# Forgetting attention: weights turned by TensorE transposes in place of a second set of logits, and a TensorE order written out by hand

## The chip, the cores and the metric

One core of one Trainium2 chip runs the whole program. The metric is the device time in microseconds (us), as a median over runs; one further execution was recorded by the hardware profiler.

## What is computed

A decoder trunk of two layers over 1024 positions of 1024 features, all in fp32: a gated linear recurrence (RG-LRU), then forgetting attention (FoX) with 16 heads of 64, each with a residual, and an RMS norm at the end. The change is in the second layer:

```python
u = h @ w_in                            # q, k, v, gate (1024 each), f_logit (16)
cum = cumsum(log_sigmoid(f_logit + b_f))            # per head, over positions
logits = (q @ k.T) / 8 + cum[query] - cum[key]      # per head, causal mask
o = softmax(logits) @ v
x = x + (o * silu(gate)) @ w_out
return rms_norm(x, final_g)
```

## The kernel before

**Number format.** Every fp32 operand is split into a high and a low part (fp32r tiles with names in h and l, by `to_hi` L72 and `to_lo` L85), and a product is three matmuls: high by high, high by low, low by high (`gemm_steps` L105). Weights arrive by DMA as `wf`; ScalarE (ACT) casts the high part `wh`, GpSimd (POOL) subtracts for the low part `wl` (`weights` L99).

**First layer** (L160 to L461). It is not touched, except that matmuls are now called through a wrapper.

**Attention, per head `hd`.** Positions are cut into two halves `c` of 512 and eight blocks of 128. `T` holds the head's keys and `U` its queries (with high part, low part and the sums `cum` stacked along the partitions, so that two matmuls give a logit with its decay); `load` L559 fills them by DMA from the projections `qkh`, `qkl`.
- `maxima(hd, c)` L631: for each of four query blocks, two to four matmuls L654 and L655 give the logits `S` (queries on partitions, keys along the free axis) in PSUM; VectorE (DVE) adds the mask and takes the negated row maximum (L659); ACT takes the exponential with that bias, in place, for the row sums alone (L662). Then the four maxima are transposed (`mrow` L668) and DVE writes them into four rows of `U` (L669), so that a second product can subtract them.
- `weigh(hd, c)` L701: for each pair of key blocks the logits are computed once more, transposed (`ST`, keys on partitions, L723 and L724), ACT takes the exponential `p` (L729, L732), POOL zeroes what lies above the diagonal (L737), DVE makes `ph` (L81) and `pl` (L86), and TensorE (PE) adds `ph` and `pl` times the values into `O` (L757, L758). A last step adds the two halves of `O` (`yo`).
- `scale`, `gated` L696, L766: POOL multiplies by the reciprocal sums (which go through DRAM, `recd` to `recb`) and by the gate.

**PSUM.** Its eight banks are two buffers for projections (tag g), two for `O`, `mrow` and `tr` (tag O), and two of two banks each (tag S), which `S` and `ST` share: every new `S` or `ST` waits until the last reader of the one before the last has ended.

**Order.** `run(order, weigh, maxima, fill)` L786 steps through a string: 0 takes a step of `weigh`, 1 a step of `maxima`, a dot a step of `fill`, which is six matmuls of the projections for the next pair of heads (`kq_units` L538, `g_units` L618; for the last heads `partial` L811, the output product of the first six pairs). ORDERS L28 holds the strings. The fill is held behind the logits of LAG steps earlier, and otherwise a scheduler in the compiler orders each engine. The engines run what they were given in that order.

**The end.** `partial` adds into the residual `x1d` in DRAM; `turned(c, q)` L827 transposes the residual with four transposes per 128x512 tile (`turn` L850), adds the last two pairs' output product (L854 to L856), and takes squares, norm and scale.

Of the kernel before, what the change touches and what calls it, by code (L numbers as in the profile page):

```python
# [38 lines left out]
def trunk(ctx: ExitStack, tc: tile.TileContext, xt, w0, wg, wo0, pc, gn, gf, w1, wv, wf, bf, wo1, out):  # L39
# [10 lines left out]


# [11 lines left out]
    for _ in range(10):  # L63
        nc.tensor.matmul(warm[:, :P], onesf, onesf, start=True, stop=True)
# [40 lines left out]
    def gemm_steps(ps, pairs, chunks=(slice(0, HALF),)):  # L105

        pairs = list(pairs)
        for cs in chunks:
            o = ps[:, cs]
            for i, ((wh, wl), (xh, xl)) in enumerate(pairs):  # L110
                nc.tensor.matmul(o, wh, xh[:, cs], start=i == 0, stop=False)  # L111
                nc.tensor.matmul(o, wl, xh[:, cs], start=False, stop=False)  # L112
                nc.tensor.matmul(o, wh, xl[:, cs], start=False, stop=i == len(pairs) - 1)  # L113
                if i % 2:
                    yield
# [12 lines left out]
    def inv_rms(parts, col, rs, rms=None):  # L128

        nb = rs.shape[1] // P  # L130
        for b, i in itertools.product(range(nb), range(len(parts))):
            sq = parts[i][:, b * P : (b + 1) * P]
            nc.tensor.matmul(col[:, b : b + 1], sq, onesf[:, :1], start=i == 0, stop=i == len(parts) - 1)
# [7 lines left out]
        inst = nc.tensor.matmul(row, onesf, rs, start=True, stop=True)  # L141
# [23 lines left out]
    with ExitStack() as l0:  # L165
# [255 lines left out]
        def mm3(o, w, x, start, stop):  # L421
            (wh, wl), (xh, xl) = w, x
            nc.tensor.matmul(o, wh, xh, start=start, stop=False)
            nc.tensor.matmul(o, wl, xh, start=False, stop=False)
            nc.tensor.matmul(o, wh, xl, start=False, stop=stop)
# [35 lines left out]
    with ExitStack() as l1:  # L461
# [4 lines left out]
        own = tu.tile([4, 4, P], BF16, name="own")  # L466
        nc.gpsimd.memset(own, 0.0)
        nc.gpsimd.affine_select(
            out=own, in_=own, pattern=[[1, 4], [0, P]], compare_op=ALU.not_equal, fill=1.0, base=0, channel_multiplier=-1
        )  # L470


# [9 lines left out]
        U = [tu.tile([P, 2, SEQ], F32R, tag=f"U{s}", name=f"U{s}") for s in range(2)]  # L482
        for s in range(2):
            nc.gpsimd.memset(f32(T[s][64:, 1]), 1.0)
            nc.vector.memset(f32(U[s][64:, 1]), 0.0)
            nc.vector.memset(f32(U[s][64:68, 1]), -1.0)

        def project(cb_i, use, hs=(0, 1)):

            w = list(weights(w1[cb_i]))  # L490
# [6 lines left out]
        def values(g):  # L497
# [9 lines left out]
            for st in range(8):  # L507
# [5 lines left out]
                for k in range(KT):  # L513
# [3 lines left out]
                    nc.tensor.matmul(pt, xh, wh, start=k == 0, stop=False)  # L517
                    nc.tensor.matmul(pt, xl, wh, start=False, stop=False)  # L518
                    nc.tensor.matmul(pt, xh, wl, start=False, stop=k == KT - 1)  # L519
# [16 lines left out]
        y1 = [[], []]  # L536

        def kq_units(pair, hs=(0, 1)):  # L538

            for is_k in (1, 0):  # L540
                if hs[0] == 0:
                    kq[pair, is_k] = tuple(
                        kqpool.tile([P, SEQ], F32R, tag=f"qk{p}{is_k}", name=f"qk{p}") for p in "hl"
                    )
                hi, lo = kq[pair, is_k]
                eng = nc.vector if pair == 0 else nc.scalar

                def use(h, pt):
                    cs = slice(h * HALF, (h + 1) * HALF)
# [7 lines left out]
                yield from project(is_k * 8 + pair, use, hs)  # L557

        def load(hd, cs=slice(0, SEQ)):  # L559

            pair, s = hd // 2, hd % 2
            rows = slice(s * HD, (s + 1) * HD)
            for is_k, A in ((1, T[s]), (0, U[s])):
                hi, lo = (f32(z[rows, cs]) for z in kq[pair, is_k])
                nc.sync.dma_start(f32(A[:64, 0, cs]), hi)
                if is_k:
                    nc.sync.dma_start(f32(A[:64, 1, cs]), hi)
                    nc.sync.dma_start(f32(A[64:, 0, cs]), lo)
                else:
                    nc.sync.dma_start(f32(A[64:, 0, cs]), hi)  # L570
                    nc.sync.dma_start(f32(A[:64, 1, cs]), lo)
            nc.sync.dma_start(f32(T[s][66:68, 1, cs]), cumd[hd, :, cs])
            nc.sync.dma_start(f32(U[s][64:66, 1, cs]), cumd[hd, :, cs])


        drain(kq_units(0, (0,)))
# [6 lines left out]
        z = at.tile([HEADS, SEQ], F32, tag="p", name="z")  # L583
        e = at.tile([HEADS, SEQ], F32, tag="p", name="e")
# [3 lines left out]
        parts = [at.tile([HEADS, SEQ], F32R, tag=t, name="cp") for t in ("ph", "pl")]  # L588

        def forget(half):  # L590
            cs = slice(half * HALF, (half + 1) * HALF)
            pt = ps.tile([P, HALF], F32, tag="O", name="fps")
            for i in range(4):
                nc.tensor.transpose(pt[:HEADS, i * P : (i + 1) * P], fz[:, half * 4 + i], ident)
            z_, e_, hi, lo = z[:, cs], e[:, cs], *(c[:, cs] for c in parts)
# [10 lines left out]
            for i in range(2):  # L606
                nc.sync.dma_start(cumd[:, i, cs], f32(parts[i][:, cs]))
            for hd in range(2):
                if half == 0:
                    load(hd, cs)  # L610
# [7 lines left out]
        def g_units(pair):  # L618

            sg = sgs[pair] = at.tile([P, SEQ], F32, tag="sg", name="sg1")  # L620
# [6 lines left out]
            yield from project(16 + pair, use)  # L627

        stats = {}

        def maxima(hd, c):  # L631

            pair, s = hd // 2, hd % 2
            if c == 0:
                stats[hd] = (
                    at.tile([P, 8], F32R, tag="st", name="st"),  # L640
                    at.tile([P, 8], F32, tag="sums", name="sums"),
                )
            st, sums = stats[hd]
            for i in range(4 * c, 4 * c + 4):
# [4 lines left out]
                qs = slice(i * P, n)  # L649
                for lo_, hi_ in ((0, min(n, HALF - o_)), (HALF - o_, n)):  # L650
                    if hi_ <= lo_:
                        continue
                    hi_ = max(hi_, lo_ + 256)
                    nc.tensor.matmul(S[:, lo_:hi_], U[s][:, 0, qs], T[s][:, 0, lo_:hi_], start=True, stop=False)  # L654
                    last[0] = nc.tensor.matmul(  # L655
                        S[:, lo_:hi_], U[s][:96, 1, qs], T[s][:96, 1, lo_:hi_], start=False, stop=True
                    )
                m = st[:, i : i + 1]
                nc.vector.tensor_tensor_reduce(  # L659
                    S[:, :n], S[:, :n], mask[:, SEQ - n :], -1.0, -NEG, ALU.add, ALU.min, accum_out=m  # L660
                )
                seen[0] = nc.scalar.activation(  # L662
                    S[:, :n], S[:, :n], AF.Exp, bias=f32(m), scale=-1.0, accum_out=sums[:, i : i + 1]
                )
                yield

            pt = ps.tile([P, P], F32, tag="O", name="mrow")
            nc.tensor.transpose(pt[:4], f32(st[:, 4 * c : 4 * c + 4]), ident)  # L668
            nc.vector.tensor_tensor(  # L669
                U[s][96:100, 1, c * HALF : (c + 1) * HALF].rearrange("p (a b) -> p a b", a=4),  # L670
                pt[:4].unsqueeze(1).to_broadcast([4, 4, P]),
                own,
                ALU.mult,
            )
            yield
# [25 lines left out]
        def weigh(hd, c, sub=slice(0, HALF)):  # L701
# [8 lines left out]
            nj = end // P  # L710
            for j0 in range(0, nj, 2):
                A = ps.tile([P, 2, HALF], F32, tag="S", name="ST")
                p = at.tile([P, 2, HALF], F32, tag="p", name="p")
                ph = at.tile([P, 2, HALF], F32R, tag="ph", name="ph")
                pl = at.tile([P, 2, HALF], F32R, tag="pl", name="pl")
                qlo = []
                for jj in range(2):
                    j = j0 + jj
                    q0 = min(max(begin, j * P), end - 256)
                    qlo.append(q0)  # L720
                    n = end - q0
                    ks = slice(j * P, (j + 1) * P)
                    nc.tensor.matmul(A[:, jj, :n], T[s][:, 0, ks], U[s][:, 0, q0:end], start=True, stop=False)  # L723
                    last[0] = nc.tensor.matmul(  # L724
                        A[:, jj, :n], T[s][:, 1, ks], U[s][:, 1, q0:end], start=False, stop=True
                    )
                ns = [end - q for q in qlo]
                if ns[0] == ns[1]:
                    nc.scalar.activation(p[:, :, : ns[0]], A[:, :, : ns[0]], AF.Exp)  # L729
                else:  # L730
                    for jj in range(2):
                        nc.scalar.activation(p[:, jj, : ns[jj]], A[:, jj, : ns[jj]], AF.Exp)  # L732
                for jj in range(2):
                    j = j0 + jj
                    w = (j + 1) * P - qlo[jj]
                    if w > 0:
                        nc.gpsimd.affine_select(  # L737
                            out=p[:, jj, :w],
                            in_=p[:, jj, :w],
                            pattern=[[1, w]],  # L740
                            compare_op=ALU.is_ge,
                            fill=0.0,
                            base=qlo[jj] - j * P,
                            channel_multiplier=-1,
                        )
                if ns[0] == ns[1]:
                    rng = [(slice(0, 2), ns[0])]
                else:
                    rng = [(jj, ns[jj]) for jj in range(2)]
                for sl, n in rng:  # L750
                    to_hi(ph[:, sl, :n], p[:, sl, :n], nc.vector)
                    to_lo(pl[:, sl, :n], p[:, sl, :n], ph[:, sl, :n], nc.vector)
# [266 lines left out]
```

## Time and profile before

| | us |
|---|---|
| median of 3 runs (1154.35 to 1156.48) | 1155.97 |
| the profiled execution's own time | 1159.8 |
| its span, first to last instruction | 1157.9 |
| PE busy | 1131.8 |
| DVE, ACT, POOL busy | 818.3, 590.7, 311.0 |

The profiled execution is 3.8 us above the median, and 1.9 us of it lie outside the span. A matmul's end is modelled, and the next one starts before it: the time that a matmul takes from the engine is therefore read from one start to the next in the timeline, not from its length. PEclk in a row of the stretches view is the granted TensorE clock, 1.00 being full speed.

### The profile page before, as it was taken

Reading aid. Unit: us, or ns where it says so; the run is one execution under the profiler, and the core shown is the slowest. Engines: PE = TensorE matmul, PEld = TensorE weight load, DVE = VectorE, ACT = ScalarE, POOL = GpSimd, SP = SyncE. Lnnn points to the kernel's source line nnn. Section 1 sums busy time; section 2 is a strip of 40 time slices with the busy share of each in tenths; the row PEclk is TensorE's granted clock in tenths of the full one; section 3 lists DMA queues with packets and bytes.
Section 4 is the critical chain, followed back from the end, with each engine's and each line's share of the span. In section 5 each row is a group of like instructions: output and inputs, shape, how many; then the busy total and the mean of one; then the engine's idle time right before and its main releaser. Section 6 shows DMA issues by size and latency. Waiting matters only on the chain.

```text
span 1157.9 us, 15580 instructions
## 1 busy us (share of the span) xinstructions
PE 1131.8 (98%) x5565; PEld 944.8 (82%) x5565; DVE 818.3 (71%) x1294; ACT 590.7 (51%) x1009; POOL 311.0 (27%) x305
## 2 busy tenths in 40 slices
PE   9999999999999999999999999999999999999897
PEld 7787888888888887978888988889888898777685
DVE  7589766677566889556877757777577775577754
ACT  8388345345544656454554545545454454445323
POOL 1212212112021103342332333323333233141310
PEclk9999999999999999999999999999999999999898
DMA  6111111111111124351343323433234331646244
GB/s 211 51 41 50 51 51 55 42 50 41 51 59 37 55 73 151 98 142 38 92 120 92 92 64 92 120 92 83 65 92 110 92 84 60 182 138 202 80 159 182
DMA packets 60221, 105.41 MB, mean 91 GB/s; under 512 B 8744, under 2 KB 23720, under 8 KB 60144
## 3 DMA queue, kind: packets, MB, share of 16 engines
q1 hardware_dynamic: 60144, 104.42, 31.9%
q8 instruction: 44, 0.72, 0.3%
q14 instruction: 33, 0.27, 0.1%
HBM read 63.30 MB, written 15.93 MB: 68 GB/s over the span
## 4 chain that ended last, share of the span: by engine, by line
PE 47%; DVE 5%; ACT 2%; DMA 2%; issue 1%; POOL 1%; DVEq 0%; SPq 0%; ACTq 0%; POOLq 0%
PE gps L111 6%; PE gps L112 6%; PE gps L113 6%; PE O L758 3%; PE ST L723 3%; PE S L655 2%; PE S L654 2%; PE ST L724 2%; PE O L757 2%; PE vps L519 2%; PE vps L517 2%; PE vps L518 2%; DVE pl L86 2%; PE ops L112 1%; PE ops L113 1%
## 5 line engine op out<-in xcount | busy, mean ns | idle before, releaser
L86 POOL TENSOR_TENSOR wl<-wf,wh 128x512 fp32r<-128x512 f32 (+2 forms) x130 | 189.0, 1458 | 504.7 <-ACT wh L75 428.6
L111 PE MATMUL gps<-hh,wh 128*128 128x512 f32 x576 | 226.8, 394 | 1.1 <-DVE qkl L555 0.7
L113 PE MATMUL gps<-hl,wh 128*128 128x512 f32 x576 | 226.7, 394 | 0.0
L112 PE MATMUL gps<-hh,wl 128*128 128x512 f32 x576 | 226.7, 394 | 0.0
L75 ACT CAST wh<-wf 128x512 fp32r<-128x512 f32 (+2 forms) x156 | 94.0, 607 | 140.1 <-PE gps L113 43.1
L662 ACT ACTIVATE S<-S,st 128x128 f32<-128x128 f32 (+7 forms) x128 | 91.4, 714 | 114.0 <-DVE st L659 112.9
L113 PEld LDWEIGHTS gps<-hl,wh 128*128 128x128 f32 x576 | 108.3, 188 | 24.3 <-issue 0.2
L111 PEld LDWEIGHTS gps<-hh,wh 128*128 128x128 f32 x576 | 108.4, 188 | 22.6 <-DVE qkl L555 1.1
L112 PEld LDWEIGHTS gps<-hh,wl 128*128 128x128 f32 x576 | 108.5, 188 | 21.6 <-issue 0.5
L86 DVE TENSOR_TENSOR pl<-p,ph 128x512 fp32r<-128x512 f32 (+2 forms) x130 | 121.7, 953 | 2.3
L81 DVE CAST ph<-p 128x512 fp32r<-128x512 f32 (+2 forms) x130 | 79.2, 619 | 57.0 <-ACT p L729 30.2
L737 POOL TENSOR_SCALAR_AFFINE_SELECT p<-p 128x128 f32<-128x128 f32 (+1 forms) x128 | 47.5, 388 | 201.6 <-ACT p L729 98.1
L659 DVE CUSTOM_DVE_ANT_0 S<-S,mask 128x128 f32<-128x128 f32 (+7 forms) x128 | 96.6, 758 | 7.1 <-PE S L655 6.2
L351 DVE TENSOR_TENSOR x<-x,ops 128x512 f32<-128x512 f32 x80 | 54.0, 681 | 50.7 <-PE ops L113 50.6
L111 PE MATMUL ups<-hh,wh 128*128 128x512 f32 x192 | 76.3, 397 | 2.6 <-DVE us L261 1.9
L113 PE MATMUL ups<-hl,wh 128*128 128x512 f32 x192 | 75.9, 395 | 0.2
L112 PE MATMUL ups<-hh,wl 128*128 128x512 f32 x192 | 75.7, 394 | 0.3 <-POOL wl L86 0.3
L758 PE MATMUL O<-pl,v 128*128 128x512 f32 (+1 forms) x198 | 67.1, 348 | 7.8 <-DVE pl L86 7.8
L729 ACT ACTIVATE p<-ST 128x512 f32<-128x512 f32 (+1 forms) x68 | 53.0, 785 | 42.4 <-PE ST L724 35.5
L518 PE MATMUL vps<-wh,hl 128*128 128x256 f32 (+1 forms) x256 | 72.7, 285 | 0.0
L517 PE MATMUL vps<-wh,hh 128*128 128x256 f32 (+1 forms) x256 | 72.6, 285 | 0.0
L519 PE MATMUL vps<-wl,hh 128*128 128x256 f32 (+1 forms) x256 | 72.4, 284 | 0.0
(192 smaller groups left out, 2517.7 us busy)
## 6 DMA issues: line engine op xcount, KB each, us to landing
wf<-in_w SPq DMA_DIRECT2D x100, 256.0 KB
wf<-in_wo SPq DMA_DIRECT2D x64, 128.0 KB
T<-qkh SPq DMA_DIRECT2D x28, 256.0 KB
U<-qkh SPq DMA_DIRECT2D x28, 256.0 KB
x<-in_xt SPq DMA_DIRECT2D x16, 256.0 KB
x1d<-x SPq DMA_DIRECT2D x16, 256.0 KB
wf<-in_wv SPq DMA_DIRECT2D x16, 256.0 KB
xp<-x1d SPq DMA_DIRECT2D x16, 256.0 KB
```

What stands on the lines that cost most here:

```text
L75: nc.scalar.copy(hi, src)
L81: eng.tensor_copy(hi, src)
L86: return eng.tensor_tensor(lo, src, f32(hi), ALU.subtract)
L111: nc.tensor.matmul(o, wh, xh[:, cs], start=i == 0, stop=False)
L112: nc.tensor.matmul(o, wl, xh[:, cs], start=False, stop=False)
L113: nc.tensor.matmul(o, wh, xl[:, cs], start=False, stop=i == len(pairs) - 1)
L517: nc.tensor.matmul(pt, xh, wh, start=k == 0, stop=False)
L518: nc.tensor.matmul(pt, xl, wh, start=False, stop=False)
L519: nc.tensor.matmul(pt, xh, wl, start=False, stop=k == KT - 1)
L659: nc.vector.tensor_tensor_reduce(S[:, :n], S[:, :n], mask[:, SEQ - n :], -1.0, -NEG, ALU.add, ALU.min, accum_out=m)
L662: seen[0] = nc.scalar.activation(S[:, :n], S[:, :n], AF.Exp, bias=f32(m), scale=-1.0, accum_out=sums[:, i : i + 1])
L758: nc.tensor.matmul(o, v, pl[:, jj, : ns[jj]], start=False, stop=j == nj - 1)
```

## The change

The exponential of `maxima` now goes to SBUF, as the weights `p` (tiles p0 to p7, one buffer each, since the two halves of a head alternate). `weigh` no longer computes logits: for each 128x128 block it transposes `p` with one fp32 transpose into PSUM (`pt`, tag S); ACT casts `ph` from there and DVE subtracts for `pl`, and the products of one pair of key blocks are issued after the transposes of the next. So `ST`, its exponential, the POOL masking, `mrow`, the four rows in `U` and DVE's cast of `ph` go. The last key block of a range is now 128 columns wide in the products with the values, where it was padded to 256.

`U` becomes three tiles of one half each: the first half's tile is shared by all heads. The fill of an even and an odd head is now 12 steps each (16 and 8 before). From head 12 on, one chain holds everything that fills: projections, loads of y, `partial`, and the first `turned`. Its y tiles are loaded straight into place and split there, and its weights' low parts move from POOL to DVE. In `run`, every PE instruction of a step is held behind the PE instruction recorded before it. At the very end, the second half's tiles are scaled after one pass that takes them out of PSUM.

The core of the diff (the wrapper, renamed tiles and plain consequences left out):

```diff
-LAG = 3
-ORDERS = (("1.10111.0.10.", "1.1010.1.0.1..10"), (".1101.1..00..11.", "111.0.0.0.11.01...."))
+ORDER = "1.0.1.1.1.0.0", "10.1.0.1.01.0.0"
+LAST = "1..0.1..1..1.0.0", "10..1.0..1.01..0..0"
...
+        U0 = tu.tile([P, 2, HALF], F32R, tag="U", name="U")
+        U = [(U0, tu.tile([P, 2, HALF], F32R, tag=f"U{s}", name=f"U{s}")) for s in range(2)]
...
+                p = ps_[i] = at.tile([P, n], F32, tag=f"p{i}", name="p", bufs=1)
                 seen[0] = nc.scalar.activation(
-                    S[:, :n], S[:, :n], AF.Exp, bias=f32(m), scale=-1.0, accum_out=sums[:, i : i + 1]
+                    p, S[:, :n], AF.Exp, bias=m, scale=-1.0, accum_out=sums[:, i : i + 1]
                 )
                 yield
-
-            pt = ps.tile([P, P], F32, tag="O", name="mrow")
-            nc.tensor.transpose(pt[:4], f32(st[:, 4 * c : 4 * c + 4]), ident)
...
+                qlo = [max(begin, j * P) for j in (j0, j0 + 1)]
...
-                    nc.tensor.matmul(A[:, jj, :n], T[s][:, 0, ks], U[s][:, 0, q0:end], start=True, stop=False)
...
+                    for q in range(qlo[jj], end, P):
+                        o = q - qlo[jj]
+                        transpose(A[:, jj, o : o + P], ps_[q // P][:, ks], ident)
...
+                    to_hi(ph, a, nc.scalar)
+                    parts.append((ph, pl))
+                for jj, (ph, pl) in enumerate(parts):
+                    to_lo(pl, A[:, jj, : ns[jj]], ph, nc.vector)
+                if held:
+                    with tc.issue_after(pe[0].ins):
+                        products(*held)
+                held = j0, qlo, parts
...
         def run(order, *gens, fill=iter(()), side=iter(())):
             for i in order:
+                with tc.issue_after(pe[0].ins):
+                    next(fill if i == "." else gens[int(i)], None)
...
-            res = tu.tile([P, 2, SEQ], F32, tag=f"{'TU'[q]}{c}", name="res")
...
+                    if c == 0 or h == 0:
+                        nc.vector.tensor_tensor(res[b][:, hs], pt, grow[:, hs], ALU.mult)
...
+                    r = root_mean(ss, lambda: nc.vector.tensor_tensor(res[b][:, hs], pt, grow[:, hs], ALU.mult))
+                    nc.scalar.activation(res[b][:, halves[0]], res[b][:, halves[0]], AF.Copy, scale=r)
...
+                    rest = [(db, c) for db in range(2, KT) for c in range(2)]
+                    fill = chain(
+                        kq_units(7),
+                        g_units(7, (0,)),
+                        load_y(0),
+                        g_units(7, (1,)),
+                        load_y(1),
+                        split_loaded(0),
+                        partial([(0, 0), (1, 0)]),
+                        split_loaded(1),
+                        partial([(0, 1), (1, 1)] + rest),
+                        turned(0, 0),
+                        turned(0, 1),
+                    )
```

The order in which the built programs hold their instructions, at two places. PE in the second run of an odd head, before: the products `O` of one pair of key blocks, the transposed logits `ST` of the next, and the turned maxima `mrow`.

```order
L758 MATMUL O<-pl,v_3760 128x512
L757 MATMUL O<-ph,v_3792 128x512
L758 MATMUL O<-pl,v_3792 128x512
L723 MATMUL ST<-U_3606,T_3604 128x512
L724 MATMUL ST<-U_3606,T_3604 128x512
L723 MATMUL ST<-U_3606,T_3604 128x384
L724 MATMUL ST<-U_3606,T_3604 128x384
L668 MATMUL mrow<-ident,st 4x128
```

PE across the end of a first run and the start of a second, in the change (L54 and L58 are the wrappers): the narrow last products of one half, a logit block of the next head, and a batch of eight transposes.

```order
L54 MATMUL O<-ph,v_3818 128x256
L689 MATMUL tr<-ident,sums 8x128
L54 MATMUL O<-pl,v_3818 128x256
L54 MATMUL O<-ph,v_3850 128x128
L54 MATMUL O<-pl,v_3850 128x128
L54 MATMUL S<-T_3599,U 128x256 x2
L58 MATMUL pt<-ident,p 128x128 x8
L54 MATMUL gps_4331<-hh,wh 128x512
```

The four `ST` matmuls of a pair of blocks have given way to a batch of single transposes, `mrow` is gone, and products of 128 columns have appeared.

DVE around the products of a head's first half, before (L659 is the row maximum, L494 takes a projection out of PSUM):

```order
L659 ISA S,st<-S,mask 128x896
L659 ISA st 128x1
L81 CAST ph<-p 128x512
L81 CAST ph<-p 128x384
L763 TENSOR_TENSOR yo<-yo,O 64x512
L86 TENSOR_TENSOR pl<-p,ph 128x512
L86 TENSOR_TENSOR pl<-p,ph 128x384
L659 ISA S,st<-S,mask 128x1024
```

The same place in the change (L673 is the row maximum, L96 the subtraction, L499 and L565 a query projection taken out of PSUM):

```order
L499 TENSOR_TENSOR gps_5088<-gps_5088,rs_3271 128x512
L673 ISA S,m<-S,mask 128x640
L673 ISA m 128x1
L751 TENSOR_TENSOR yo<-yo,O 64x512
L565 SCALAR_TENSOR_TENSOR qkl<-gps_5088,qkh 128x512
L96 TENSOR_TENSOR pl<-pt,ph 128x512
L96 TENSOR_TENSOR pl<-pt,ph 128x384
L673 ISA S,m<-S,mask 128x768
```

The casts `ph` have left DVE, and `pl` now reads the transposes in PSUM, not `p` in SBUF; a projection's two passes stand ahead of it.

More of the change, by code (lines that the diff above doesn't have):

```diff
@@ L63, in trunk @@
     for _ in range(10):
-        nc.tensor.matmul(warm[:, :P], onesf, onesf, start=True, stop=True)
+        matmul(warm[:, :P], onesf, onesf, start=True, stop=True)
     pct = const.tile([P, 8, NB], F32, name="pct")
@@ L132, in inv_rms @@
             sq = parts[i][:, b * P : (b + 1) * P]
-            nc.tensor.matmul(col[:, b : b + 1], sq, onesf[:, :1], start=i == 0, stop=i == len(parts) - 1)
+            matmul(col[:, b : b + 1], sq, onesf[:, :1], start=i == 0, stop=i == len(parts) - 1)
         if rms is None:
@@ L140, in inv_rms @@
         row = ps.tile([P, HALF], F32, tag="O", name="rsrow")[:, : nb * P]
-        inst = nc.tensor.matmul(row, onesf, rs, start=True, stop=True)
+        inst = matmul(row, onesf, rs, start=True, stop=True)
         nc.scalar.copy(rs, row)
@@ L710, in weigh @@
             nj = end // P
-            for j0 in range(0, nj, 2):
[L712 to L716, printed above, removed]
-                for jj in range(2):
[L718 to L732, printed above, removed]
-                for jj in range(2):
[L734 to L752, printed above, removed]
-                for jj in range(2):
-                    j = j0 + jj
-                    v = V[j][:, 2 * s : 2 * s + 2].rearrange("p a d -> p (a d)")
-                    o = O[:, qlo[jj] - begin :]
-                    nc.tensor.matmul(o, v, ph[:, jj, : ns[jj]], start=j == 0, stop=False)
-                    nc.tensor.matmul(o, v, pl[:, jj, : ns[jj]], start=False, stop=j == nj - 1)
@@ L811, in partial, with pair_of_y, split_y @@
-        def partial():
-            ws = {}
-            for db, c in [(0, 0), (1, 0), (0, 1), (1, 1)] + [(db, c) for db in range(2, KT) for c in range(2)]:
-                if db not in ws:
-                    ws[db] = list(weights(wo1[db, :, :6]))
-                x = at.tile([P, HALF], F32, tag="xp", name="xp", bufs=3)
+        def pair_of_y(c, pair):
+            y1[c][pair] = tuple(hpool.tile([P, HALF], F32R, tag=t, name="y" + t) for t in ("hh", "hl"))
+            return y1[c][pair]
+        def split_y(c, pair, y, sub=slice(0, HALF)):
+            yh, yl = (z[:, sub] for z in (pair_of_y(c, pair) if sub.start == 0 else y1[c][pair]))
+            to_hi(yh, y, nc.scalar)
+            to_lo(yl, y, yh, nc.vector)
@@ new lines, in load_y, with split_loaded, partial @@
+        def load_y(c):
+            for pair in range(6):
+                nc.sync.dma_start(f32(pair_of_y(c, pair)[1]), y1d[c, pair])
+            yield from ()
+        def split_loaded(c):
+            for pair in range(6):
+                yh, yl = y1[c][pair]
+                to_hi(yh, f32(yl), nc.scalar)
+                to_lo(yl, f32(yl), yh, nc.vector)
+            yield from ()
+        def partial(todo):
+            for db, c in todo:
+                if db not in wo:
+                    wo[db] = list(weights(wo1[db, :, :6], lo_eng=nc.vector))
+                x = rpool.tile([P, HALF], F32, tag="R", name="xp")
@@ L937, in trunk @@
             if hd + 2 < HEADS:
-                load(hd + 2)
+                load(hd + 2, us=(0,) if hd % 2 == 0 and hd < 12 else (0, 1))
         quarters = [slice(0, 256), slice(256, HALF)]
```

261 lines of the change are left out of this document (133 added, 128 removed).

## The prediction

> **What bounds the kernel now.** I read the page's busy times first.
>
> ```profile
> span 1157.9 us, 15580 instructions
> PE 1131.8 (98%) x5565; PEld 944.8 (82%) x5565; DVE 818.3 (71%) x1294; ACT 590.7 (51%) x1009; POOL 311.0 (27%) x305
> ```
>
> PE is busy 98% of the span and no other engine above 71%. So only two things can move the time: what PE has to do, and where it waits. I take the waits from the view of who waited for whom, on PE, and the stretches around the longest of them and at the end.
>
> ```profile
> PE O L758 <- DVE pl L86: 7.8, 5, 3.8
> PE turn L850 <- ACT sq L860: 2.5, 1, 2.5
> PE ST L723 <- ACT S L662: 1.6, 2, 1.2
> ...
> 550.00:1000.00 450.00, 447.14 (x2411) 385.33 (x2410) 322.34 (x607) 223.33 (x457) 155.95 (x172) 1.00 0.37 93
> 1070.00:1076.00 6.00, 2.79 (x16) 2.14 (x15) 6.00 (x1) 2.21 (x5) 5.48 (x6) 0.98 0.17 54
> 1076.00:1081.00 5.00, 4.38 (x10) 3.48 (x11) 4.94 (x12) 1.18 (x3) 1.53 (x3) 0.50 0.49 154
> 1115.00:1146.00 31.00, 30.60 (x179) 25.78 (x177) 15.84 (x31) 12.61 (x33) 2.11 (x4) 1.00 0.48 165
> 1149.00:1152.50 3.50, 2.43 (x10) 1.53 (x10) 2.97 (x6) 1.34 (x6) 0.00 (x0) 0.76 0.33 121
> ```
>
> A row of waits gives the sum, the number of times and the longest; a row of stretches has the busy time of PE, weight load, DVE, ACT and POOL, and then PE's clock. From 550 to 1000 us, in the attention heads, PE lacks 2.9 us of 450: that stage is bound by its work. The waits are 7.8 us for `pl` and a few more towards the end, and the longest (3.8 us) is followed by 5 us at a clock of 0.50, which costs 2.5 us more.
>
> **PE's work.** What one matmul takes is read in the timeline from its start to the next start. Columns: start, length, engine, line.
>
> ```profile
> 1060.17 0.28 PE L757 MATMUL O<-ph,v 128*128 128x256 f32 x1
> 1060.29 0.28 PE L758 MATMUL O<-pl,v 128*128 128x256 f32 x1
> 1060.41 0.39 PE L112 MATMUL ops<-yhh,wl 128*128 128x512 f32 x1
> 1060.64 0.40 PE L113 MATMUL ops<-yhl,wh 128*128 128x512 f32 x1
> 1060.88 0.34 PE L654 MATMUL S<-T,U 128*128 128x384 f32 x1
> 1061.05 0.34 PE L655 MATMUL S<-T,U 96*128 96x384 f32 x1
> 1061.23 0.40 PE L111 MATMUL ops<-yhh,wh 128*128 128x512 f32 x1
> ...
> 1131.94 0.61 PE L850 MATMUL turn<-ident,x 128*128 128x128 f32 x4
> 1132.31 0.48 PE L854 MATMUL turn<-woh,yhh 128*128 128x512 f32 x1
> 1132.62 0.39 PE L855 MATMUL turn<-woh,yhl 128*128 128x512 f32 x1
> ...
> 451.57 1.02 PE L141 MATMUL rsrow<-rs,onesf 128*128 128x512 f32 x2
> 452.02 0.79 PE L423 MATMUL ops<-yh,wh 128*128 128x512 f32 x1
> 452.65 0.40 PE L424 MATMUL ops<-yh,wl 128*128 128x512 f32 x1
> ```
>
> 512 columns take 0.235 us, 384 take 0.175, 256 take 0.12. Four fp32 transposes and one matmul of 512 take 0.68 us (1131.94 to 1132.62), so a transpose takes 0.11. A plain fp32 matmul of 512 columns (two instructions, `rsrow`) takes 452.65 - 451.57 - 0.23 = 0.85.
>
> ```profile
> L723 PE MATMUL ST<-U,T 128*128 128x512 f32 x91 | 37.3, 409 | 1.3 <-ACT S L662 1.2
> L723 PE MATMUL ST<-U,T 128*128 128x384 f32 x31 | 10.4, 336 | 0.0
> L723 PE MATMUL ST<-U,T 128*128 128x256 f32 x76 | 20.3, 286 | 0.5 <-ACT S L662 0.4
> L668 PE MATMUL mrow<-ident,st 128*4 128x128 f32 x32 | 8.7, 271 | 0.0
> ```
>
> - Removed: `ST`, twice (L723 and L724): 2 x (91 x 0.235 + 31 x 0.175 + 76 x 0.12) = 71.8 us; and 32 `mrow` at 0.11 = 3.5 us.
> - Added: 36 transposes a head (blocks on and below the diagonal), 576 x 0.11 = 63.4 us.
> - Changed: 66 products `O` (33 last key blocks, `ph` and `pl`) go from 256 to 128 columns. No row has an fp32r matmul below 256 columns. The lower bound is the transpose's 0.11 us, which also loads weights and streams 128 columns: -0.7 us in all. The upper is the 512-column row's 0.235: +7.6. I take the plain fp32 rate, 0.85 / 4 = 0.21, since the fast rate is shown only from 256 columns up and the data is the same four bytes: +5.9.
>
> Sum: -71.8 - 3.5 + 63.4 + 5.9 = **-6.0 us**. The logits turn out to be little dearer than the transposes.
>
> **Waits that go.** Why was `pl` late? The view of the tiles, and the timeline of DVE and POOL at the longest wait:
>
> ```profile
> L86 DVE TENSOR_TENSOR pl<-p,ph x130: 544/692/7002, 529.3 to 1124.8; 128x512 fp32r<-128x512 f32 x69, 128x384 fp32r<-128x384 f32 x31, 128x1024 fp32r<-128x1024 f32 x30
> L86 DVE TENSOR_TENSOR qkl<-gps,qkh x16: 672/690/692, 462.9 to 974.0; 128x512 fp32r<-128x512 f32 x16
> ...
> 1069.46 2.39 POOL L699 TENSOR_TENSOR sg<-sg,recb 64x1024 f32<-64x1024 f32 x1 [14.22 <-DMA recb<-recd]
> 1072.30 3.18 POOL L86 TENSOR_TENSOR wl<-wf,wh 128x512 fp32r<-128x512 f32 x3
> 1069.56 7.00 DVE L86 TENSOR_TENSOR pl<-p,ph 128x1024 fp32r<-128x1024 f32 x1
> ```
>
> One `pl` took 7.00 us while POOL was busy nearly all the time; the lengths of `pl`, whose operands are both in SBUF, run up to ten times the median. `qkl` at the same line reads PSUM and never exceeds 692 ns. In the change `pl` reads PSUM like `qkl`, so I expect it to be free of that: -7.8 us of waits, and -2.5 us of low clock behind the longest. The 1.6 us of `ST` waiting for the exponential of `S` goes with `ST`; what takes its place is next.
>
> **Waits that come.** The strict order makes PE stand wherever an operand is late. In each head the tightest places are where `pt` takes over the tag-S buffer of the `pt` before it. That buffer is free after two casts on ACT and two subtractions on DVE, one behind the other.
>
> ```profile
> L75 ACT CAST qkh<-gps 128x512 fp32r<-128x512 f32 x14 | 8.2, 588 | 17.8 <-DVE gps L494 17.5
> L662 ACT ACTIVATE S<-S,st 128x1024 f32<-128x1024 f32 x16 | 17.4, 1088 | 13.9 <-DVE st L659 13.7
> L662 ACT ACTIVATION_READ_ACCUMULATOR S<-S,st 128x1 f32 x128 | 24.8, 194 | 0.1
> L659 DVE CUSTOM_DVE_ANT_0 S<-S,mask 128x1024 f32<-128x1024 f32 x16 | 19.6, 1228 | 0.3 <-PE S L655 0.2
> L659 DVE DVE_READ_ACCUMULATOR2_ANT st<- 128x1 fp32r x128 | 16.8, 131 | 0.4
> ```
>
> With the qkh and qkl rows: 2 x 0.59 + 2 x 0.69 = 2.56, and some 0.3 for the hand-overs (an estimate): 2.9 us. The order "10.1.0" puts between the two batches a dot (6 x 0.235 = 1.41), a logit block (2 x 0.12) and a dot: 3.06 us. So it fits, barely. The longest logit block needs 1.23 + 0.13 + 1.09 + 0.19 + 0.3 = 2.9 us before its buffer is free, and the next user but one comes after two dots and a block of 0.3 or more, 3.1 us or more. With nothing else in the queues no such place waits; each head has about four with under 0.5 us to spare, and a neighbour's 0.69 us can cost a part of that. I take 0.2 us a head, 16 x 0.2 = **+3.2**; the bounds are 0 and, with every one of the four late by 0.25, 16.
>
> The end: in `turned(1, .)` the second half of a two-bank tile waits for the first half's square and its pass on DVE, since they are one tile: 0.6 (a 512-wide ACT pass, as qkh) + 0.19 + 0.69 + 0.3 = 1.8 us, twice: 3.6. Before, it was 2.5 us once and 3.5 us at a clock of 0.76 (0.8 us lost): **+0.3**. In the last quarter a chain of narrower casts (two of each, an estimate of 1.8 us from these rows) stands behind the squares of `turned` against a cover of 2.2 us: **+1.0**, from 0 to 3.
>
> What the rest costs nothing and why: ACT's cast of `ph` replaces its exponential of `ST` on the same columns; POOL's masking goes, off PE's path; the low parts of the output weights on DVE (16 subtractions, none over the 0.69 us of the qkl row, 11 us at most) are spread over the last heads, and DVE is 71% busy over the span. The loads of `U` become twice as many DMAs of half the size on SP's queue; every one is needed a whole run (14 us of PE work) after its source. If DVE's cover is gone, the price is the same 0.69 us steps as above.
>
> **Sum**: -6.0 - 7.8 - 2.5 - 1.6 + 3.2 + 0.3 + 1.0 = -13.4 us on the profiled execution's 1159.8: 1146.4. The median of the runs is 3.8 us lower than that execution, so the forecast is 1156.0 - 13.4 = **1142.6**, rounded 1143.
>
> **Rivals.**
> - *Narrow products at the fast rate.* The 66 products cost 0.11 and not 0.21: 6.6 us less, 1136. For it: nothing but the even slope of the 256, 384 and 512 rows; against it: no row below 256.
> - *The strict order puts DVE's projection passes in the chain (slower).* Where a projection's two passes stand in the queue ahead of `pl` (as the order of DVE shows once a run) and come late, a chain of 2.9 us becomes 2.9 + 2 x 0.69 = 4.3 against a cover of 3.06: 1.2 us. At one place a head it costs 16 x 1.2 = 19 us in place of 3.2: 1159. At two places, 1178. It decides from 1.05 us of waits a head (16.6 us of gains / 16). For it: before, other work could slip in front of a late product, now it can't. Against it: those passes stand at the widest gap (some 4 us), and DVE, busy 322 of 450 us in that stage, loses a cast for each `pl`.
> - *The waits stay.* `pl` was not late because of POOL, or the new splits are caught instead: 7.8 + 2.5 + 1.6 are not won, 1155. Against it: the qkl row, and the splits are wanted a whole matmul group later. (The Trainium skill, page "SBUF — State Buffer", section "Who interferes with whom": a GpSimd operation and a VectorE operation with two SBUF inputs exclude each other for a whole instruction. By that rule the new VectorE splits of output weights and loaded y, with both inputs in SBUF, stay exposed; the 7.00 us row agrees.)
> - *Transposes let the clock fall.* A batch of eight is 0.9 us; if each were followed by 5 us at half clock, as the wait of 3.8 us was, 96 batches would cost 240 us: 1383. Against it: the stretch from 1115 to 1146, with four to six transposes in a row every 1.8 us, ran at a clock of 1.00. (The Trainium skill, "TensorE: Matmul & The Clock Gate", part on PE-mode transpose, says that full clock does not engage for transposes; the row speaks against that here, where matmuls stand between.)
>
> **How the numbers follow.** The forecast's case has 0.55, the fast narrow products 0.20, the waits that stay 0.06, the slower rival 0.17, the clock 0.02. A measurement of this kernel can tell about 0.2% (2.3 us) from no change. Faster: 0.55 + 0.20 + a third of 0.06 = 0.77; within 0.2%: 0.04; slower: 0.19. The range goes from the fast products without new waits (1136 - 3 = 1133) to the forecast with the upper bound of waits (1143 + 12.8 + 2 = 1158).
>
> **What would show it.** In the changed profile: `pt` from start to start 0.11 us; the 128-column `O` 0.21; no wait for `pl` above 1 us and `pl` never above 0.8 us long; no stretch of low clock before the last tiles; waits of `S` and `pt` for ACT and DVE of some 3 us in all; two waits of 1.8 us on `turn`. The prediction is wrong if PE's waits on tag S exceed 16 us, or if a transpose takes longer in a batch of eight than in four.

## The result, and the profile after

The change makes no difference that can be measured: 1156.12 us as a median of 12 runs (1153.60 to 1159.94), against 1155.88 for the kernel before on the same chip (12 runs, 1154.35 to 1158.66). The ratio is 1.0002, with a 95% interval of 0.9989 to 1.0016. The forecast of 1143 was wrong: a gain of 13 us did not come. The profiled execution of the change took 1156.1 us.

The page's busy times, the waits of PE and three stretches, of the change:

```profile
span 1154.1 us, 15825 instructions
PE 1121.8 (97%) x5713; PEld 942.8 (82%) x5713; DVE 723.0 (63%) x1222; ACT 593.2 (51%) x1081; POOL 230.1 (20%) x159
```

```profile
PE ops L54 <- ACT yhh L85: 8.9, 1, 8.9
PE turn L54 <- DVE res L869: 4.6, 2, 2.7
PE vps L54 <- POOL wl L96: 3.7, 4, 1.1
PE ups L54 <- DVE us L271: 1.9, 1, 1.9
PE turn L54 <- DMA x<-x1d: 1.9, 1, 1.9
...
PE vps L54 <- ACT wh L85: 1.0, 3, 0.3
```

```profile
550.00:1000.00 450.00, 446.41 (x2558) 388.59 (x2557) 250.11 (x542) 227.61 (x513) 105.45 (x72) 1.00 0.37 97
1018.40:1023.00 4.60, 4.51 (x16) 3.67 (x17) 3.85 (x7) 2.71 (x7) 0.00 (x0) 0.56 0.00 0
1108.00:1116.00 8.00, 5.96 (x29) 4.81 (x29) 2.68 (x6) 2.43 (x7) 0.72 (x1) 0.79 0.26 86
```

PE is busy 10 us less, so work did go. The waits for `pl` and `ST` are gone. In their place stand other waits: 8.9 us, once, for the high part of a loaded `y`, 4.7 us on the values' product `vps` and 1.9 us for the reloaded `x`, none of which has a term in the forecast's sum, and 4.6 us on `turn`, which the prediction had named at 3.6. The 8.9 us are followed by 4.6 us at a clock of 0.56, which costs 4.51 x 0.44 = 2.0 us more; behind the wait for `x` the same arithmetic gives 1.3.

**Where the 8.9 us come from.** The timeline of the change; first the other engines and SP's queue, then PE:

```profile
1005.18 0.28 DVE L691 COPY rc<-tr 8x128 f32<-8x128 f32 x1 [0.54 <-PE tr L689]
...
1006.98 0.68 SPq L692 DMA_DIRECT2D recd<-rc  x1
...
1009.37 0.47 SPq L696 DMA_DIRECT2D recb<-recd  x1
...
1013.59 2.34 POOL L705 TENSOR_TENSOR sg<-sg,recb 64x1024 f32<-64x1024 f32 x1 [38.42 <-DMA recb<-recd]
...
1016.00 1.26 POOL L760 TENSOR_TENSOR yo<-yo,sg 128x512 f32<-128x512 f32 x1
1017.30 0.62 ACT L85 CAST yhh<-yo 128x512 fp32r<-128x512 f32 x1 [6.18 <-POOL yo L760]
1017.82 1.66 ACT L85 CAST yhh<-yhl 128x512 fp32r<-128x512 f32 x3
...
1018.49 0.79 PE L54 MATMUL ops<-yhh,wh 128*128 128x512 f32 x1 [8.85 <-ACT yhh L85]
```

Read it from the bottom. PE wants `yhh` of the loaded `y` (the cast `yhh<-yhl`), for `partial` (0, 1). That `y` had long been loaded: SP issued the last load of a `y` (L799) at 993.0, and PE stands from 1009.6. But ACT stood 6.18 us before another cast, `yhh<-yo` of pair 6, which is ahead of it in ACT's order. That one waits for POOL, POOL for the reciprocal sums, and these make two trips through DRAM (`recd`, `recb`) between 1006.98 and 1013.59, after 1.5 us in SP's queue. The six casts of the loaded `y` (the row shows the three that began before its view ends) could have run at any time in those 6 us, and stood behind one that waited for the longest chain of the head. (The Trainium skill, "TensorE: Matmul & The Clock Gate", Part 1, architectural detail: ACT and DVE take their instructions strictly in order. The 6.18 us row agrees.)

### The profile page after: what moved, and what is told of

It reads as the page before. It is cut to its first block, busy times and chain, and to the rows that moved or that the text cites. A ratio compares the mean times of both kernels' runs of the same rounds, so it can differ in the third digit from the quotient of the medians.

```text
span 1154.1 us, 15825 instructions
## 1 busy us (share of the span) xinstructions
PE 1121.8 (97%) x5713; PEld 942.8 (82%) x5713; DVE 723.0 (63%) x1222; ACT 593.2 (51%) x1081; POOL 230.1 (20%) x159
## 4 chain that ended last, share of the span: by engine, by line
PE 86%; DVE 4%; issue 3%; DMA 3%; POOL 2%; ACT 2%; SPq 0%; POOLq 0%; ACTq 0%; DVEq 0%
PE gps L54 31%; PE ops L54 16%; PE ups L54 11%; PE vps L54 6%; PE S L54 6%; PE O L54 5%; PE pt L58 5%; PE gate L54 3%; PE turn L54 2%; DMA recb<-recd 1%; POOL sg L705 1%; POOL wl L96 1%; DMA recd<-rc 1%; DVE sq L162 1%; DVE hl L238 1%
## 5 line engine op out<-in xcount | busy, mean ns | idle before, releaser
L96 POOL TENSOR_TENSOR wl<-wf,wh 128x512 fp32r<-128x512 f32 (+1 forms) x114 | 166.2, 1463 | 664.3 <-ACT wh L85 472.2
L54 PE MATMUL gps<-hh,wh 128*128 128x512 f32 x576 | 228.9, 398 | 0.2 <-DVE qkl L565 0.2
L54 PE MATMUL gps<-hh,wl 128*128 128x512 f32 x576 | 226.7, 394 | 0.1
L54 PE MATMUL gps<-hl,wh 128*128 128x512 f32 x576 | 226.7, 393 | 0.0
L678 ACT ACTIVATE p<-S,m 128x128 f32<-128x128 f32 (+7 forms) x128 | 94.8, 741 | 141.1 <-DVE m L673 139.7
L96 DVE TENSOR_TENSOR pl<-pt,ph 128x512 fp32r<-128x512 f32 (+1 forms) x198 | 98.8, 541 | 101.6 <-ACT ph L85 101.1
L54 PEld LDWEIGHTS gps<-hl,wh 128*128 128x128 f32 x576 | 108.2, 188 | 24.5
L54 PEld LDWEIGHTS gps<-hh,wl 128*128 128x128 f32 x576 | 108.7, 189 | 20.4 <-POOL wl L96 0.6
L54 PEld LDWEIGHTS gps<-hh,wh 128*128 128x128 f32 x576 | 108.5, 188 | 20.0 <-DVE qkl L565 0.4
L673 DVE CUSTOM_DVE_ANT_0 S<-S,mask 128x128 f32<-128x128 f32 (+7 forms) x128 | 97.4, 762 | 40.5 <-PE S L54 39.0
L85 ACT CAST ph<-pt 128x512 fp32r<-128x512 f32 (+1 forms) x198 | 83.0, 474 | 28.9 <-PE pt L58 23.5
L54 PE MATMUL S<-T,U 96*128 96x512 f32 (+7 forms) x384 | 92.1, 349 | 0.0
L58 PE MATMUL pt<-ident,p 128*128 128x128 f32 x576 | 80.0, 275 | 0.0
L54 PEld LDWEIGHTS S<-T,U 128*128 128x128 f32 (+1 forms) x384 | 69.1, 190 | 13.2 <-ACT p L678 0.8
L54 PE MATMUL ups<-hh,wh 128*128 128x512 f32 x192 | 76.7, 400 | 2.5 <-DVE us L271 1.9
L58 PEld LDWEIGHTS pt<-ident,p 128*128 128x128 f32 x576 | 69.2, 142 | 10.7 <-issue 0.4
L54 PE MATMUL ups<-hl,wh 128*128 128x512 f32 x192 | 76.5, 398 | 0.2
L54 PE MATMUL ops<-yh,wh 128*128 128x512 f32 x192 | 76.1, 396 | 0.5 <-DVE x L453 0.5
L54 PE MATMUL vps<-wl,hh 128*128 128x256 f32 (+1 forms) x256 | 72.8, 286 | 3.7 <-POOL wl L96 3.7
L54 PE MATMUL ups<-hh,wl 128*128 128x512 f32 x192 | 76.0, 396 | 0.0
```

The source lines that it names most:

```text
L54: pe[0] = nc.tensor.matmul(*args, **kw)
L58: pe[0] = nc.tensor.transpose(*args)
L85: nc.scalar.copy(hi, src)
L96: return eng.tensor_tensor(lo, src, f32(hi), ALU.subtract)
L673: nc.vector.tensor_tensor_reduce(S[:, :n], S[:, :n], mask[:, SEQ - n :], -1.0, -NEG, ALU.add, ALU.min, accum_out=m)
L678: seen[0] = nc.scalar.activation(p, S[:, :n], AF.Exp, bias=m, scale=-1.0, accum_out=sums[:, i : i + 1])
```

## Experiments

Times are medians where more than one run is named; the kernel before, run beside them, had medians of 1155.1 to 1155.6, and ratios are to it.

### before_again: the kernel before, unchanged

> The kernel before, unchanged, for a second profile. If the 3.8 us wait for one subtraction (7.00 us long, with POOL busy beside it) is part of every execution, PE's waits on pl come to about 7.8 us again and the span to about 1158. If it was a matter of chance in how POOL and DVE met, the longest wait on pl is under 2 us and the span nearer to 1154, so that the profile of before that was shown was some 4 us above a usual execution.

One execution, 1156.82 us. PE's three largest waits, and two stretches:

```profile
PE O L758 <- DVE pl L86: 2.8, 4, 0.8
PE ST L723 <- ACT S L662: 2.8, 3, 2.1
PE turn L850 <- ACT sq L860: 2.5, 1, 2.5
```

```profile
1008.00:1012.00 4.00, 4.00 (x12) 3.23 (x12) 1.64 (x3) 1.62 (x4) 0.00 (x0) 0.57 0.64 174
1146.00:1148.50 2.50, 2.50 (x8) 1.82 (x6) 2.41 (x4) 0.00 (x0) 0.00 (x0) 0.52 0.49 182
```

The wait of 3.8 us, and the low clock behind it, aren't in this execution; its longest `pl` took 3.67 us, not 7.00. It has low clock in other places instead, behind the wait of 2.1 us for `S` and near the end: 1.7 + 1.2 = 2.9 us lost. So part of what the prediction wanted to win was one execution's chance.

### split_early: the six loaded casts ahead of pair 6's

```diff
                         split_loaded(0),
-                        partial([(0, 0), (1, 0)]),
+                        partial([(0, 0)]),
                         split_loaded(1),
+                        partial([(1, 0)]),
                         partial([(0, 1), (1, 1)] + rest),
```

> The change, with the split of the second half's loaded y recorded one output block earlier, so that it no longer stands in ACT's queue behind the cast that waits for POOL. Theory (a queue blocked at its head): the 8.9 us wait of PE goes, with the 2.0 us lost in 4.6 us at a clock of 0.56 behind it: about 1145, ratio to before 0.990 to 0.992. Rival (the loads of y or the splits themselves are late): the wait only moves or shrinks to 4 or 5 us, about 1151. Rival (another wait takes its place, since ACT still stands for 6 us): within 3 us of 1156.

1148.14 us (1144.64 to 1149.94, 6 runs), ratio 0.9929 (0.9914 to 0.9945). From POOL's and ACT's timeline:

```profile
1013.39 2.40 POOL L705 TENSOR_TENSOR sg<-sg,recb 64x1024 f32<-64x1024 f32 x1 [39.26 <-DMA recb<-recd]
1015.88 1.62 POOL L760 TENSOR_TENSOR yo<-yo,sg 128x512 f32<-128x512 f32 x1
```

```profile
1017.53 0.62 ACT L85 CAST yhh<-yo 128x512 fp32r<-128x512 f32 x1 [2.92 <-POOL yo L760]
```

PE's longest wait is now one on `turn`:

```profile
PE turn L54 <- DVE res L869: 4.5, 2, 2.6
```

The chain through DRAM ends when it did (1017.53 against 1017.30), yet PE no longer waits for `yhh`. The length of the chain was not the fault; what stood behind it was. The median misses the 1145 of the theory by 3 us. The six executions go from 1144.64 us at a mean granted clock of 0.999 to 1149.94 at 0.992, and the profile is of the fastest: so the rest goes with low clock in the others, at places that no profile shows.

### turn_banks: one bank for each turned half

```diff
-                    if c == 1 and b == 1:
-                        if h == 0:
-                            two = two_banks("turn")
-                        pt = two[:, h]
-                    else:
-                        pt = ps.tile([P, HALF], F32, tag="gO"[c * q], name="turn")
+                    pt = ps.tile([P, HALF], F32, tag="gO"[c * b], name="turn")
```

> The change, with the last four tiles of the second half in four single banks, two of each tag, in place of two halves of one two-bank tile. If the second half of such a tile waits for the passes over the first half only because they are one tile, the two waits of 2.7 and 1.9 us on turn go: 4.6 us less, about 1151.5. If the wait is really for ACT and DVE, which are late at the end anyway, the time stays within 1.5 us of 1156 and the wait goes to the tail.

1150.75 us (1146.67 to 1152.26, 5 runs), ratio 0.9961 (0.9948 to 0.9975). The first two rows of PE's waits:

```profile
PE ops L54 <- ACT yhh L85: 8.1, 1, 8.1
PE vps L54 <- POOL wl L96: 2.6, 3, 0.9
```

The row of `turn` waiting for `res` is gone and the wait for `yhh` is not. The 4.6 us were on the path. (The edit also moves the first two of the second column block's four tiles from tag O to tag g.)

### order_free: the strict order taken away

```diff
             for i in order:
-                with tc.issue_after(pe[0].ins):
-                    next(fill if i == "." else gens[int(i)], None)
+                next(fill if i == "." else gens[int(i)], None)
...
-                    with tc.issue_after(pe[0].ins):
-                        products(*held)
+                    products(*held)
```

> The change without the strict order: nothing holds a step's TensorE instructions behind the one recorded before, so the scheduler places them. The trace shows no PE wait on the S and pt tiles under the strict order, so if the order itself costs nothing the time is 1156 or more, and slower by up to 15 us where the scheduler puts products ahead of late operands. Rival (the strict order is what gave the gain back): 1145 to 1150.

1204.32 us, ratio 1.0423 (1.0409 to 1.0436).

```profile
PE O L54 <- DVE pl L96: 15.1, 20, 1.5
PE pt L58 <- ACT p L678: 8.8, 12, 1.4
PE O L54 <- ACT ph L85: 6.7, 13, 1.1
PE S L54 <- ACT p L678: 6.6, 9, 0.8
```

Without the order by hand, PE waits at every link of the heads' chain: 54 times in these rows, for up to 1.5 us, 37 us in all. None of these four waits is in the change. The order is worth 48 us in this kernel: the opposite of the slower rival. All of PE's waits together are 27.5 us more than in the change, and some 8 us more go to low clock; the rest of the 48 was not followed up. The edit also leaves the fill without the looser hold (LAG) that it had in the kernel before, so 48 us is not what the strict order gains over that one.

### values_lows_dve: the values' low parts on DVE

```diff
-                parts += split_weights(src, (2, 256 + ex), nc.scalar, nc.gpsimd)
+                parts += split_weights(src, (2, 256 + ex), nc.scalar, nc.gpsimd if ex else nc.vector)
```

> The change with one edit: the low parts of the values' weights (attention heads alone) are made on DVE in place of POOL. If PE's four waits for wl (3.7 us in all) come from POOL's slow subtractions, three of the four go and some 1.2 us at each of three value blocks with them: about 2.5 to 3.5 us less, 1152.5. If DVE, whose queue there holds the row maxima and the subtractions of the transposes, makes them as late or makes the heads' own passes late instead, the time stays at 1155 or rises, with PE waits for pl or S in place of those for wl.

1155.35 us (12 runs), ratio 0.9994 (0.9982 to 1.0006): no gain. Two of PE's waits:

```profile
PE vps L54 <- DVE sg L644: 2.1, 3, 0.7
...
PE vps L54 <- POOL wl L96: 1.0, 1, 1.0
```

Three of the four waits for POOL went. Three for DVE's pass over the gate came (2.1 us), and three for the low parts themselves, now on DVE (0.7): the low parts had hidden another late operand.

### rest_order: another order of the last partial products

```diff
-                    rest = [(db, c) for db in range(2, KT) for c in range(2)]
+                    rest = [(db, c) for db in range(2, 6) for c in range(2)] + [(6, 0), (7, 0), (6, 1), (7, 1)]
```

> The change with one edit: the last partial products of the output projection run in the order (6,0), (7,0), (6,1), (7,1) in place of (6,0), (6,1), (7,0), (7,1). If the 1.9 us that PE waits for the reloaded x of the first turned tile is a matter of what stands between its producer and it, a different order moves the wait by at most the length of one group (some 2 us) either way: 1154 to 1158, and the 8.9 us wait for yhh stays. If it is a cover that only wants the right order, 1.9 us of wait and 1.7 us of low clock go: 1151.5.

1158.21 us (12 runs), ratio 1.0020 (1.0009 to 1.0031).

```profile
PE turn L54 <- DVE yhl L96: 2.0, 1, 2.0
...
PE turn L54 <- DMA x<-x1d: 0.9, 1, 0.9
```

The wait for the reloaded residual halved, but the first turned tile now comes before its `yhl`. This edit moves the wait and gains nothing.

### both_fixes and all_fixes

both_fixes joins turn_banks with the same order of ACT as split_early, by recording pair 6's split one run later (head 13's `gated(hd, 0)` moves behind the second run):

```diff
             scale(hd)
-            gated(hd, 0)
+            if hd != 13:
+                gated(hd, 0)
...
             drain(side)
+            if hd == 13:
+                gated(hd, 0)
             gated(hd, 1)
```

> The change with two edits at once: the split of pair 6's first half is recorded after the six casts of the loaded y (ACT's queue then as in split_early), and the turned tiles of the second column block are single banks with a buffer each (as in turn_banks). If the two waits are separate places on PE's path, their gains add: split_early was 7.0 below the kernel before and turn_banks 4.3 below it, the unedited change level with it, so 1155 - 7.0 - 4.3 = about 1144 (ratio 0.990), with no wait for yhh and none of turn on the multiplication. If they hide each other (a wait removed early only lets PE arrive earlier at the next late operand), it stays near split_early's 1148.

1142.02 us (1138.35 to 1143.15, 4 runs), ratio 0.9878 (0.9856 to 0.9900): the gains add, and this beats both kernels by 1.2%. Its profiled execution is the fastest of the four; its span, and the largest of PE's waits in it:

```profile
span 1136.4 us, 15824 instructions
```

```profile
PE vps L54 <- POOL wl L96: 3.1, 4, 0.9
```

all_fixes adds rest_order and values_lows_dve to it.

> The change with all four edits (the split order, single turned banks, the order of the last partial products, the values' low parts on DVE). If every one of the waits named is a place of its own on PE's path, the gains add: 1144 for the first two, less 2.5 to 3.5 for the values and up to 3.6 for the first turned tile: 1137 to 1141 (ratio 0.985 to 0.988). If the last two edits only move waits, it equals both_fixes, near 1144.

1143.46 us (1142.64 to 1144.74, 4 runs), ratio 0.9888 (0.9869 to 0.9907): the last two edits only move waits here too.

### wide_last: the narrow products 256 wide

```diff
                 for j, q, (ph, pl) in zip((j0, j0 + 1), qlo, parts):
+                    if end - q < 256:
+                        q, (ph, pl) = end - 256, parts[0]
```

> The change with its 66 products of 128 columns made 256 columns wide again; they are given the preceding key block's weights, so the output holds that block twice and the last block not at all, and only the time counts. If a product of 128 columns cost the plain fp32 rate of 0.21 us, as the prediction took it, 256 columns at 0.12 would be cheaper: 66 x (0.12 - 0.21) = -5.9 us, 1150 (ratio 0.995). If it costs what the trace of the change shows from start to start (0.060 us ahead of another narrow one, 0.11 ahead of a wider one, 0.085 on average), the time rises by 66 x 0.035 = 2.3 us, 1158 (ratio 1.002). If narrow products cost the price of wide ones because something else bounds that place, it stays at 1156.

1155.12 us (12 runs), ratio 0.9992 (0.9977 to 1.0007), against the change's 1.0002: no difference that can be told, so neither 1150 nor 1158. The two timelines show why, at the same one of the 33 places. The change:

```profile
704.97 0.36 PE L54 MATMUL O<-pl,v 128*128 128x256 f32 x1
705.17 0.22 PE L54 MATMUL O<-ph,v 128*128 128x128 f32 x1
705.23 0.28 PE L54 MATMUL O<-pl,v 128*128 128x128 f32 x1
705.34 0.45 PE L54 MATMUL S<-T,U 128*128 128x256 f32 x2
705.63 1.04 PE L58 MATMUL pt<-ident,p 128*128 128x128 f32 x8
```

wide_last:

```profile
703.60 0.36 PE L54 MATMUL O<-pl,v 128*128 128x256 f32 x1
703.80 0.28 PE L54 MATMUL O<-ph,v 128*128 128x256 f32 x1
703.92 0.28 PE L54 MATMUL O<-pl,v 128*128 128x256 f32 x1
704.03 0.40 PE L54 MATMUL S<-T,U 128*128 128x256 f32 x2
704.28 1.04 PE L58 MATMUL pt<-ident,p 128*128 128x128 f32 x8
```

From start to start the narrow products take 0.06 and 0.11 us, 0.17 together; 256 columns wide they take 0.23. But the two logit matmuls behind them take 0.29 in the change and 0.25 here. The whole stretch, from the first row to `pt`, is 0.66 us with narrow products and 0.68 with wide ones. Narrowing wins 0.06 us and loses two thirds of it in what comes next. With the two traces laid side by side, the stretch up to the end of that successor differs by 0.03 us at most at each of the 33 places. My expectation of 2.3 us had priced the pair and not its successor. Why the successor is slower was not tried.

### transposes_twice: every transpose made twice

```diff
                         transpose(A[:, jj, o : o + P], ps_[q // P][:, ks], ident)
+                        transpose(A[:, jj, o : o + P], ps_[q // P][:, ks], ident)
```

> The change with each of the 576 transposes of the attention weights made twice, into the same place: nothing else. If a transpose costs 0.109 us from start to start at full clock, wherever it stands, the time rises by 576 x 0.109 = 62.8 us, to 1219 (ratio 1.054), with the clock over the attention heads still 1.00; where PE now waits (the 8.9 us) nothing is absorbed, as no head's transposes stand there. If batches of sixteen let the clock fall, as the rival has it, the rise is well above 70 us and the records show a granted clock below 0.95 in the heads. If part of the transposes lies in time that PE has over anyway, it is below 55 us.

1219.53 us (4 runs), ratio 1.0546 (1.0524 to 1.0568), which is 63 us above the change.

```profile
550.00:1000.00 450.00, 446.41 (x2737) 396.46 (x2736) 222.47 (x486) 206.07 (x465) 99.21 (x68) 1.00 0.32 80
```

576 more transposes cost 0.11 us each, and with batches of up to sixteen the clock over the heads is 1.00.

## Why the prediction was wrong, point by point

- **PE's work: -6.0 forecast, about -11.9 by these runs.** The transposes cost what was forecast. The term for the 66 narrow products was mis-sized: +5.9 forecast, about 0 by wide_last. The guess that the fast rate ends at 256 columns was wrong, and even the lower bound, 0.11 us for each, is above what they take (0.17 us for two); the rival of fast narrow products was nearer. This error alone would have made the change faster than forecast.
- **Waits that go: 11.9 forecast (7.8 + 2.5 + 1.6).** They went: `pl`, which now reads PSUM, is never above 0.69 us long (7.00 before), and PE never waits for it.

```profile
L96 DVE TENSOR_TENSOR pl<-pt,ph x198: 279/548/693, 523.1 to 1122.3; 128x512 fp32r<-128x512 f32 x91, 128x256 fp32r<-128x256 f32 x43, 128x128 fp32r<-128x128 f32 x33, 128x384 fp32r<-128x384 f32 x31
```

  But the size came from one execution. before_again had 2.8 us of waits for `pl` and 2.8 for `ST`, with 1.7 us of low clock behind one of these: 7.3. And the forecast took 11.9 from the median of the runs, while the execution that showed them was 3.8 us above that median. That no `pl` is slow any more fits the argument on POOL; it was not tried alone.
- **The steady waits of the strict order: +3.2 forecast, 0 found.** No `S` and no `pt` waits in the change. Order_free shows that the order is what keeps them away; the slower rival falls.
- **The end: +0.3 and +1.0 forecast.** The two waits on `turn` were seen and named (3.6 forecast, 4.6 found; turn_banks gives them back). The change's only other named cost, the narrower casts of the last quarter, has no wait of its own in the profile.
- **The step that failed** stands in two places of the prediction: "What the rest costs nothing", whose list of free edits has the low parts of the output weights on DVE but not the splits of the loaded `y`, with their casts on ACT, and the rival of the waits that stay. That rival named it ("the new splits are caught instead") and was set aside because "the splits are wanted a whole matmul group later". That judged when a split is wanted, not what stands ahead of it in ACT's queue. The orders shown ahead of the prediction are those of PE and DVE; the order of ACT, which decided, is not among them. It cost 8.9 us of waiting and 2.0 of low clock; split_early, where nothing else is changed, gives 7 to 8 us back, and its profiled execution 11.4. That the rival's 1155 is near the measured 1156 is partly luck: the waits for `pl`, which it counted as kept, did go.
- **Also not foreseen:** the values' 4.7 us and the 1.9 us for the reloaded `x`. Two edits aimed at them only moved them; what would remove them stays open.

The sum closes on the profiles of before_again and the change: all PE waits together are 16.5 and 25.6 us (+9.1), time lost to low clock, added up over the stretches, 3.0 and 5.2 (+2.2, of which 1.6 is a dip at 50 us, in the first layer, that the change does not touch apart from its wrapper), work -11.9. That makes -0.6; the spans differ by -0.8. For both_fixes, which lost nothing to low clock while PE worked, the same sum is 13.4 - 16.5 - 3.0 - 11.9 = -18.0, and its span is 18.5 below. That its median is near the forecast is no merit of the forecast: other terms add up to that number.

## What to carry to other kernels

When a change puts an operation into an engine's in-order queue, ask not only how long it takes and when it is wanted, but what the instruction ahead of it waits for; a cast that waits for a trip through DRAM stops every free cast behind it. Read the order of that engine at that place before costing the edit at nothing. Waits seen in one execution are a sample: before they are counted as gains, look for them in a second one. And a wait that is cured by an edit shows whether it was the path only in the time: two of four edits here shortened a wait or took it out of the table, and won no time.

## What the runs showed of the hardware

- A matmul of 128 columns in the fast fp32 form starts the next after 0.06 us where that one is narrow too, and after 0.11 us ahead of a logit matmul. There is no fall to the plain rate (0.21) below 256 columns, but the two logit matmuls behind such a pair take 0.29 us in place of 0.25, so narrowing below 256 gained nothing that could be measured here.
- Half the clock can follow a wait of 2 us. In before_again a wait of 2.07 us, in the change one of 1.92, was followed by some 4 us near half clock; the change's waits of 2.66 and 1.93 us on `turn`, which end at 1136.57 and 1146.14, were not:

```profile
1125.00:1137.00 12.00, 9.34 (x53) 7.40 (x51) 8.13 (x17) 6.27 (x17) 0.73 (x1) 1.00 0.57 206
1137.00:1150.00 13.00, 9.26 (x49) 7.03 (x46) 5.15 (x15) 6.07 (x17) 0.00 (x0) 1.00 0.46 174
```

  (The Trainium skill, "TensorE: Matmul & The Clock Gate", Part 1: the clock falls after an idle window of about 3.4 us, and the windows run freely. The runs differ in the length: less than 2 us sufficed.) Nor is it the length alone, or the code at that place. The first layer's wait for `us`, the same code in the change, split_early and both_fixes, is 1.94 us in each; the clock fell behind it in the change's profile and stayed at 1.00 from 48 to 54 us in the other two:

```profile
48.00:54.00 6.00, 5.19 (x16) 4.15 (x17) 4.77 (x5) 4.17 (x4) 1.29 (x1) 0.72 0.15 48
```

  What decides it beside the length was not tried.
